# TensorE in place of SyncE waits, behind its loop, until a batched matmul's stores are complete

## The chip, the core and the metric

The kernel runs on one core of a Trainium2 chip. The metric is the device time of one execution in microseconds (us), and less is better. A core has five engines with an instruction stream each: TensorE (PE, with its weight loads shown as PEld), VectorE (DVE), ScalarE (ACT), GpSimd (POOL) and SyncE (SP), which in this kernel issues every DMA. The engines meet only through semaphores. An execution ends when all five are through.

## The reference

The kernel multiplies 32 pairs of float32 matrices: x[b] is 256 by 512 and y[b] is 512 by 384.

```python
batch, dim_i, dim_j, dim_k = 32, 256, 512, 384
return np.einsum('bij,bjk->bik', x, y).astype(np.float32)
```

It reads 41.94 MB and writes 12.58 MB.

## The kernel before

**Tiling.** The 32 matrices are worked off as N = 8 groups of Q = 4. A group lies in SBUF with 32 partitions for each of its four matrices. TensorE multiplies in float16, 32 rows by 128 columns at a time, so that the four matrices of a group use four bands of the array. Each group is done in NE = 2 halves of the rows of x, and each half is 16 steps (T = 16) of four products. Eight banks of PSUM hold the results of both halves.

**Who does what.** SyncE loads group n+2 of x (L69) and y (L73) when GpSimd has cast the same buffer's earlier group. GpSimd casts x and y to float16 (L126, L136). VectorE transposes x (L156) and takes five of sixteen blocks of each result half from PSUM to SBUF (L165); ScalarE takes the other eleven (L165). TensorE runs two nested hardware loops, over the 8 groups and over their 2 halves (L231, L232); the products stand at L217, and each wait in them is a `take` (L214), a wait that also takes the counted value back from its semaphore.

**Stores.** All results have a place of their own in SBUF, and SyncE stores them in three pieces (L96): groups 0 to 4, groups 5 and 6, and group 7. The third piece waits for the last copies of ScalarE and VectorE (L108 and the line behind it). Each store adds 16 to the semaphore s_out when its data has landed.

**The end.** The streams are written out by hand, engine by engine. Behind its third store SyncE raises s_sp (L110), and GpSimd, which waits for it, sets the program's other semaphores to zero (L145) and is through. SyncE's last instruction waits until s_out has 48, and takes the 48 back (L111):

```python
    store(N - 1, N)
    sp.sem_inc(s_sp, 1)
    sp.wait_op(s_out, 16 * 3, "sem-ge").then_inc(s_out, -16 * 3)
```

VectorE and ScalarE end with their last copy, TensorE with the branch of its outer loop. No instruction of the program brings the five engines together at its end.

Of the kernel before, what the change touches and what calls it, by code (L numbers as in the profile page):

```python
# [19 lines left out]
def kernel(  # L20
# [41 lines left out]
    s_out = nc.alloc_semaphore("s_out")  # L62
# [28 lines left out]
    sp = nc.sync  # L91
# [16 lines left out]
    sp.wait_ge(s_dve, NE)  # L108
    store(N - 1, N)
    sp.sem_inc(s_sp, 1)  # L110
    sp.wait_op(s_out, 16 * 3, "sem-ge").then_inc(s_out, -16 * 3)  # L111

# [96 lines left out]
    te = nc.tensor  # L211

    def take(sem):
        te.wait_op(sem, 1, "sem-ge").then_inc(sem, -1)  # L214

    def product(ps, w, m, start, stop, g):
        return te.add_instruction(  # L217
            mybir.InstMatmult(
                name=nc.get_next_instruction_name(),
                start_tensor_calc=start,  # L220
                stop_tensor_calc=stop,
                tile_size=(PQ, P),
                tile_position=(PQ * g, 0),
                engine=mybir.EngineType.PE,
                ins=[te.lower_ap(m), te.lower_ap(w)],
                outs=[te.lower_ap(ps)],
            )
        )

    xt = xt_sb.bitcast(MM_DT).rearrange("p t (m c) -> p t m c", c=2)  # L230
    with te.Fori(0, N):  # L231
        with te.Fori(0, NE) as e:  # L232
            take(s_act)
            take(s_dve)
            for t in range(T):
                if t % STEP == 0:
                    take(s_yr)
                    take(s_xt)
                for g in range(Q):
                    s = slice(g * PQ, (g + 1) * PQ)  # L240
                    ins = product(
                        o_ps[:, e * Q + g, :K],
                        xt[s, t // 2, :, t % 2],
                        y_r[s, t],
                        t == 0,
                        t == T - 1,
                        g,
                    )
                    if t == T - 1 or (g == Q - 1 and t % STEP == STEP - 1):
                        ins.then_inc(s_pe, 1)  # L250


# [28 lines left out]
```

## Time and profile before

| what | value |
|---|---|
| device time, median of 3 runs | 131.95 us (131.85 to 132.28) |
| the profiled execution's own time | 132.13 us |
| its span, first to last instruction of the program | 130.8 us |
| mean granted TensorE clock | 0.823 |
| DMA, mean over the span | 417 GB/s |
| busy: TensorE, VectorE, ScalarE, GpSimd | 47%, 63%, 64%, 57% of the span |

The profile is one execution. Its span runs from the first to the last instruction that belongs to the program; the device time also holds what the engines do around the program, and the two differ by 1.33 us here. Waits, branches and DMA issues are instructions of an engine's sequencer (its name is then PEldq, SPq, ACTq and so on), and they don't count as busy. A wait's start is the moment when it was released. The page cuts the span into 40 slices of about 3.3 us; a digit is a busy share in tenths.

### The profile page before, as it was taken

Reading aid. Unit: us, or ns where it says so; the run is one execution under the profiler, and the core shown is the slowest. Engines: PE = TensorE matmul, PEld = TensorE weight load, DVE = VectorE, ACT = ScalarE, POOL = GpSimd, SP = SyncE. Lnnn points to the kernel's source line nnn. Section 1 sums busy time; section 2 is a strip of 40 time slices with the busy share of each in tenths; the row PEclk is TensorE's granted clock in tenths of the full one; section 3 lists DMA queues with packets and bytes.
Section 4 is the critical chain, followed back from the end, with each engine's and each line's share of the span. In section 5 each row is a group of like instructions: output and inputs, shape, how many; then the busy total and the mean of one; then the engine's idle time right before and its main releaser. Section 6 shows DMA issues by size and latency. Waiting matters only on the chain. (4 is left out here: it accounts for less than half of the span.)

```text
span 130.8 us, 3199 instructions
## 1 busy us (share of the span) xinstructions
PE 61.4 (47%) x1024; PEld 46.7 (36%) x1024; DVE 82.7 (63%) x144; ACT 84.1 (64%) x178; POOL 74.2 (57%) x42
## 2 busy tenths in 40 slices
PE   0000009910992589089329905980975499100000
PEld 0000009800991566046129604970953236000000
DVE  0000036899379999985997997599999957920000
ACT  0400000599659989993998899399999957994000
POOL 0006991199929965992899459758973970000000
PEclk9999999995589689977986985599599959965555
DMA  5999999999999999999999999999999999999995
GB/s 120 451 396 441 421 431 451 443 408 428 451 413 421 438 443 401 436 436 443 423 458 398 443 408 466 398 418 436 463 398 408 427 438 425 436 428 421 425 440 248
DMA packets 3379, 54.55 MB, mean 417 GB/s; under 512 B 304, under 2 KB 304, under 8 KB 304
## 3 DMA queue, kind: packets, MB, share of 16 engines
q1 hardware_dynamic: 3376, 54.53, 98.1%
q14 instruction: 3, 0.02, 0.0%
HBM read 41.94 MB, written 12.58 MB: 417 GB/s over the span
## 5 line engine op out<-in xcount | busy, mean ns | idle before, releaser
L165 ACT COPY o_sb<-o_ps (+1 forms) x176 | 82.6, 469 | 31.7 <-PE o_ps L217 29.6
L217 PE MATMUL o_ps<-y_r,xt_sb 32*128 32x384 f16 x1024 | 61.4, 384 | 50.4 <-PEq L214 49.5
L217 PEld LDWEIGHTS o_ps<-y_r,xt_sb 32*128 32x128 f16 x1024 | 46.7, 107 | 64.6 <-issue 56.8
L156 DVE STREAM_TRANSPOSE xt_sb<-x_r 128x256 f32<-128x256 f32 x64 | 38.1, 626 | 30.9 <-POOL x_r L126 18.4
L136 POOL CAST y_r<-y_sb 128x1536 f16<-128x1536 f32 (+1 forms) x22 | 44.3, 2049 | 15.8 <-DMA y_sb<-in_y_dram 15.3
L165 DVE COPY o_sb<-o_ps 32x384 f32 (+1 forms) x80 | 44.6, 557 | 1.6
L126 POOL CAST x_r<-x_sb 128x2048 f16<-128x2048 f32 x16 | 30.2, 1893 | 16.8 <-DVE o_sb L165 12.1
L202 ACT ACT_TABLE_LOAD x1 | 1.3, 1283 | 3.4 <-PEq L78 3.4
L265 POOL MEMSET const-float32-0.0<- 128x1 f32 x1 | 0.1, 98 | 0.2 <-issue 0.2
L202 ACT COPY spare<-const-float32-0.0 1x1 f32<-1x1 f32 x1 | 0.2, 190 | 0.0
L265 POOL MEMSET const-bfloat16-1.0<- 128x1 bf16 x1 | 0.1, 101 | 0.0
L265 POOL MEMSET const-uint8-127<- 128x1 uint8 x1 | 0.1, 101 | 0.0
L265 POOL MEMSET const-float32-1.0<- 128x1 f32 x1 | 0.1, 98 | 0.0
## 6 DMA issues: line engine op xcount, KB each, us to landing
y_sb<-in_y_dram SPq DMA_DIRECT2D x8, 3072.0 KB, 16.8
x_sb<-in_x_dram SPq DMA_DIRECT2D x8, 2048.0 KB, 17.0
out_dram<-o_sb SPq DMA_DIRECT2D x1, 7680.0 KB, 33.9
out_dram<-o_sb SPq DMA_DIRECT2D x1, 3072.0 KB, 17.3
out_dram<-o_sb SPq DMA_DIRECT2D x1, 1536.0 KB, 11.5
```

The lines of the kernel that those rows point to most:

```text
L126: po.tensor_copy(x_r[:, e], x_sb[n % 2][:, e * H : (e + 1) * H]).then_inc(s_cast, 1)
L136: ins = po.tensor_copy(y_r[:, s], y_sb[n % 2][:, s])
L156: v.transpose(xt_w[:, w], words[:, e, w]).then_inc(s_xt, 1)
L165: ins = copy(o_sb[g * PQ : (g + 1) * PQ, n, e, h], o_ps[h * PQ : (h + 1) * PQ, e * Q + g, :K],)
L202: a_.copy(spare, nc.const_aps.tensor(0.0, [1, 1], F32))
L217: return te.add_instruction(mybir.InstMatmult(name=nc.get_next_instruction_name(), start_tensor_calc=start, stop_tensor_calc=stop, tile_si ...
L265: nc = _bacc.Bacc("TRN2", target_bir_lowering=False, num_devices=1)
```

## The change

SyncE's last instruction is taken away, and the same wait, with the same value and the same taking back, is put behind TensorE's two loops. SyncE then ends with the raising of s_sp, and GpSimd's clearing stays as it is.

```diff
     store(N - 1, N)
     sp.sem_inc(s_sp, 1)
-    sp.wait_op(s_out, 16 * 3, "sem-ge").then_inc(s_out, -16 * 3)
...
                     if t == T - 1 or (g == Q - 1 and t % STEP == STEP - 1):
                         ins.then_inc(s_pe, 1)
+    te.wait_op(s_out, 16 * 3, "sem-ge").then_inc(s_out, -16 * 3)
```

The last line stands outside both loops and runs once.

## The prediction

> **What bounds the kernel now.** I read the page first: its span, its slices and its DMA rows.
>
> ```profile
> span 130.8 us, 3199 instructions
> ...
> PE   0000009910992589089329905980975499100000
> ...
> PEclk9999999995589689977986985599599959965555
> DMA  5999999999999999999999999999999999999995
> ...
> q1 hardware_dynamic: 3376, 54.53, 98.1%
> ```
>
> The DMA row is the one to read: 9 in every slice but the first and the last, while TensorE's row is 0 in the last five. The queue's packets took 98.1% of the span of sixteen DMA engines. The kernel is bound by moving its 54.53 MB, and the change moves no byte and no issue of a DMA. So it can only touch the end. For the end I read the stretches of the tail:
>
> ```profile
> core 0: us, PE busy (x) PEld busy (x) DVE busy (x) ACT busy (x) POOL busy (x), PEclk, DMA share, GB/s
> ...
> 105.90:119.30 13.40, 5.82 (x96) 3.14 (x96) 7.25 (x13) 10.86 (x24) 1.13 (x1) 0.75 1.00 427
> 119.30:130.80 11.50, 0.00 (x0) 0.00 (x0) 0.00 (x0) 0.00 (x0) 0.00 (x0) 0.50 0.89 380
> ```
>
> From 119.3 us on no engine computes; the DMA share is 0.89 and the granted clock of TensorE 0.50. The last 11.5 us are the third store. SyncE's own waits say who stands there:
>
> ```profile
> SPq L111 <- SPq L111: 11.1, 1, 11.1
> SPq L108 <- DVE o_sb L165: 5.0, 1, 5.0
> ```
>
> The longest of the end is SyncE's 11.1 us at L111, the wait that moves. The page's chain of work ends with a ScalarE copy at 119.2 us and doesn't show this; the waits of the DMA queue's own engine do. The lines around it, one by one:
>
> ```profile
> L111 SPq EVENT_SEMAPHORE  x1: 17/17/17, 130.8 to 130.8; - x1
> ```
>
> ```profile
> L110 SPq EVENT_SEMAPHORE  x1: 17/17/17, 119.7 to 119.7; - x1
> ```
>
> ```profile
> L96 SPq DMA_DIRECT2D out_dram<-o_sb x3: 345/390/403, 85.9 to 119.3; - x3
> ...
> DMA to landing us min/median/max: 11.5/17.3/33.9
> ```
>
> The three stores are issued by 119.3, s_sp is raised at 119.7, and SyncE's last wait is released at 130.8 and takes 17 ns. It is the last instruction of the span. The profiled execution's own time is 132.13 us, so 1.33 us lie around the span. Who arrives there when is what the change alters.
>
> **The change part by part.** *Taken from SyncE:* one wait of 17 ns at the very end. SyncE is then through at 119.7 us, 11.1 us sooner. Nothing is queued behind it, and the landing of the stores doesn't depend on it.
>
> *Added to TensorE:* the same wait behind its loops. When does TensorE come to it?
>
> ```profile
> L231 PEldq ALU_OP  x8: 36/36/36, 25.6 to 110.6; - x8
> L231 PEldq COMPARE_BRANCH  x8: 76/208/214, 25.7 to 110.6; - x8
> ```
>
> ```profile
> L217 PEld LDWEIGHTS o_ps<-y_r,xt_sb x1024: 90/93/148, 19.4 to 111.3; 32*128 32x128 f16 x171
> L217 PE MATMUL o_ps<-y_r,xt_sb x1024: 318/322/523, 19.4 to 111.4; 32*128 32x384 f16 x171
> ```
>
> The last branch of the outer loop starts at 110.6, and the last products start at 111.4 and take 0.32 us. These products were handed over ahead of the branch, so the wait stands behind them and holds nothing up; no instruction of the program is queued behind it. TensorE waits there for about 20 us, in which it had nothing to do anyway. What a wait costs on TensorE stands in its loop, with SyncE beside it at the opening barrier:
>
> ```profile
> L214 PEldq EVENT_SEMAPHORE  x160: 51/51/51, 3.9 to 109.9; - x160
> ```
>
> ```profile
> L265 SPq EVENT_SEMAPHORE  x1: 17/17/17, 0.7 to 0.7; - x1
> L265 ACTq EVENT_SEMAPHORE  x1: 17/17/17, 0.7 to 0.7; - x1
> L265 DVEq EVENT_SEMAPHORE  x1: 21/21/21, 0.7 to 0.7; - x1
> L265 PEldq EVENT_SEMAPHORE  x1: 51/51/51, 0.7 to 0.7; - x1
> ```
>
> 160 waits of TensorE take 51 ns each, the least as much as the most, through stretches with a granted clock of 1.00 and of 0.50. SyncE's take 17. So the end of the span moves by 51 - 17 = 34 ns. Two times of the trace's semaphore records, which no view prints, add to this. A semaphore's last rise and the start of the wait that it releases lie 17 ns apart for SyncE at L111 (130,767 and 130,784 ns) and 28 or 29 ns for TensorE in its loop (for instance 107,069 for a rise at 107,041): 11 ns more. **First term: 34 + 11 = 45 ns**, inside the span.
>
> *What comes behind the span.* The semaphore records go on after it. Semaphore 2 isn't the program's; it rises in the opening and at the end. Its rises near the end, in ns from the span's start, from the trace's records:
>
> ```
> 111912 119360 120402 120446 130937 130981 131020 131054 131101
> 131895 131929 131967 132011 132035 132133 132171 132206 132252
> ```
>
> Between the two rows of nine, from 131,063 to 131,671, some 230 other semaphores change once each: they are set back. I read each row as a barrier through which the five engines go one by one, up and back: five steps up, four back. The first row says who is who. TensorE's last product raised its semaphore at 111,751, and 111,912 is the first step. ScalarE's last copy raised its own at 119,256, and 119,360 is the second. GpSimd's clearing starts at 119.7 and takes 163 ns:
>
> ```profile
> L145 POOLq EVENT_SEMAPHORE_RANGE_CLEAR  x1: 163/163/163, 119.7 to 119.7; - x1
> ```
>
> and 120,402 is the third. The fourth, 44 ns later, is then VectorE, which had been through since 115.2. The fifth, at 130,937, is SyncE, 136 ns after its wait ended at 130,801. So the order is TensorE, ScalarE, GpSimd, VectorE, SyncE, and back. SyncE comes last in this order **and** last in time: four steps back are all that is left, 131,101 - 130,937 = 164 ns. If TensorE, the first in the order, comes last in time, the other four still have to step behind it. The second row shows such a full pass, since there everybody waits for TensorE's first step: 132,252 - 131,895 = 357 ns. **Second term: 357 - 164 = 193 ns.** Its bounds are 0, if the order is not what I read, and 357.
>
> *TensorE's way from its wait to the barrier.* SyncE needed 136 ns. TensorE never did just this, so I bound it. From the end of the wait to the next signal at the program's own barriers (L78, semaphore 96) TensorE needed 121 ns (3,100 to 3,221) and SyncE 83 (3,054 to 3,137): 38 ns more, or 1.46 times as much, 174 to 198 ns. From its last product's rise to its barrier step it needed 161 ns, from a standing start. The far row is GpSimd's, 537 ns from the clearing's end (119,865) to 120,402. I take 186, next to the rows of TensorE's own: **third term: 186 - 136 = 50 ns**, with ends at 25 and 401.
>
> The setting back that follows is the same work. Its last part runs until 131,671 on the semaphores 8 to 53, after TensorE is let go at 131,101, and TensorE's step opens the second barrier. TensorE is let go last before and after, so this part shifts and doesn't change.
>
> **The sum:** 45 + 193 + 50 = 288 ns, or 0.29 us, 0.22%. Against the profiled execution: 132.13 + 0.29 = 132.42, with a span of 130.85. The profiled execution is 0.18 above the median of the runs shown; on the median it is 131.95 + 0.29 = **132.24 us**.
>
> The Trainium skill, "Runtime: NRT & Kernel Launch", section "The ~15µs preamble/postamble breakdown", has a serpentine barrier over five engines at 44 ns a step, eight steps, 355 ns. The trace agrees, with 357. By its even steps the second term would be 4 x 44 = 176 ns and the sum 0.27 us.
>
> What can be told from no change in this kernel is about 0.3%, 0.4 us. My forecast is a small loss below that.
>
> **The rivals.** *A, the other side: slower by over 0.3%.* The mechanism is TensorE's way from its wait to its barrier step. It decides from 0.40 - 0.045 - 0.193 = 0.16 us more than SyncE's 0.136, that is from about 0.30 us. If it were as long as GpSimd's 537 ns, the third term would be 401 ns and the sum 0.64: 132.59 us. For it: every instruction of TensorE's sequencer that can be compared is slower than SyncE's (51 to 17, 121 to 83). Against it: at 111,912 TensorE made this very step 161 ns after its last product. What speaks half for it is that part of this way may have been done beside the products, between 110.7 and 111.7.
>
> *B: only the span's 45 ns count.* The device time might stop ahead of the barrier's steps, or the order might not be what I read. Then it is 131.95 + 0.05 = 132.00. For it: I don't know where in the records the 1.33 us begin and end. Against it: with 130.8 of span and 132.13 in all, the clearing of semaphores (to 131.67) and most of the second barrier fit inside.
> [...]
>
> *C: faster.* SyncE may have closing work of its own that now lies beside the third store. From its wait's end to the end of the first setting back by the semaphores 207 to 255, which follow its step, are 131,151 - 130,801 = 350 ns. If TensorE cost nothing and all of this had been on the path, 131.60. Against it: SyncE's share ends ahead of the last one, at 131,671, so hiding it brings nothing.
>
> *D: the change doesn't do what it says*, if TensorE's wait were inside a loop or passed early. The diff has it behind both loops, and s_out reaches 48 only with the third store; if it passed early, TensorE's end would stand near 111 us and the span at 119.9.
>
> **How the numbers follow.** Forecast, a loss of 0.2 to 0.4 us: 0.60, of which about 0.07 are measured beyond 0.4, since the runs of before alone spread over 0.43 us. A: 0.22. B: 0.13, within 0.3%. C: 0.05, of which 0.04 beyond 0.3%. D: well below 0.01, left out of the count. So faster 0.04, within 0.3% 0.53 + 0.13 + 0.01 (the rest of C) = 0.67, slower 0.07 + 0.22 = 0.29. The range reaches from B's 132.00, less 0.10 for the low end of the runs shown (131.85 against 131.95), which is 131.90, to A's 132.59 with as much on top, 132.70; C and the far ends of A stay out.
>
> **What would show it.** In the changed profile TensorE's wait should be the last instruction, of 51 ns, some 28 ns behind the last rise of s_out, and SyncE's last one the raising of s_sp. Between its end and the first of the last nine-step pass I expect 186 ns, and the first pass should last about 357 ns with TensorE's step first and late. The profiled time less the span should grow from 1.33 to about 1.57 us. DMA's row should be the same, digit for digit nearly. If the store's landing moves by more than a few tenths, it is noise of the transfers, not the change. I am wrong if the pass is no longer than 164 ns (the order is read wrongly) or if TensorE's way to it is over 0.30 us.

## The result, and the profile after

The changed kernel takes 132.39 us (median of 10 runs, 132.23 to 133.0) against 131.95 us before (131.85 to 132.28). The ratio is 1.0035, with a 95% interval of 1.0024 to 1.0046: slower by 0.32 to 0.61 us. The profiled execution took 132.25 us, with a span of 130.6 us. Its page, with the rows that were shown of before:

```profile
span 130.6 us, 3199 instructions
...
PE   0000009920992589089419944990985399200000
...
PEclk9999999995589689977985699599599959965555
DMA  5989999999999999999999999999999999999996
...
q1 hardware_dynamic: 3376, 54.53, 98.2%
```

The DMA row is full again in all but its ends and one slice at 8, and the queue's share is 98.2% (98.1% before): the stretch that bounds the kernel is the same. The tail, as stretches:

```profile
core 0: us, PE busy (x) PEld busy (x) DVE busy (x) ACT busy (x) POOL busy (x), PEclk, DMA share, GB/s
...
105.90:119.30 13.40, 5.85 (x96) 3.15 (x96) 7.30 (x13) 11.04 (x24) 1.16 (x1) 0.75 1.01 431
119.30:130.60 11.30, 0.00 (x0) 0.00 (x0) 0.00 (x0) 0.00 (x0) 0.00 (x0) 0.50 0.89 381
```

No engine computes behind 119.3 us, at the same clock and the same DMA share of 0.89. SyncE's own waits have lost their row of 11.1 us:

```profile
SPq L108 <- DVE o_sb L164: 4.9, 1, 4.9
SPq L96 <- ACT o_sb L164: 4.1, 1, 4.1
```

What SyncE ends with, what TensorE ends with, and the stores, by line (the change shifts the lines of TensorE's loop by one):

```profile
L110 SPq EVENT_SEMAPHORE  x1: 17/17/17, 119.7 to 119.7; - x1
```

```profile
L250 PEldq EVENT_SEMAPHORE  x1: 51/51/51, 130.6 to 130.6; - x1
```

```profile
L96 SPq DMA_DIRECT2D out_dram<-o_sb x3: 345/389/403, 86.3 to 119.3; - x3
...
DMA to landing us min/median/max: 11.3/17.1/33.4
```

And the rows that say when TensorE came to its wait, its outer loop's branch and its waits within the loop, and when GpSimd was through:

```profile
L230 PEldq COMPARE_BRANCH  x8: 76/208/214, 25.8 to 110.7; - x8
```

```profile
L213 PEldq EVENT_SEMAPHORE  x160: 51/51/51, 3.8 to 109.9; - x160
```

```profile
L216 PE MATMUL o_ps<-y_r,xt_sb x1024: 318/321/523, 19.5 to 111.5; 32*128 32x384 f16 x171
```

```profile
L144 POOLq EVENT_SEMAPHORE_RANGE_CLEAR  x1: 161/161/161, 119.7 to 119.7; - x1
```

TensorE left its loop at 110.7 us, its last products started at 111.5 (111.4 before), its waits take the same 51 ns, and GpSimd cleared the other semaphores at 119.7 as before. SyncE is through at 119.7. TensorE's wait, 51 ns long, is the last instruction, at 130.6. The third store takes 11.3 us to land, against 11.5, and starts at the same 119.3. So the span is not longer in this execution, it is shorter by 0.16 us (130,801 to 130,645 ns), since the store landed earlier. And yet the time is 0.12 us longer: what lies around the span went from 1.33 to 1.60 us. The records of semaphore 2 in the changed kernel, in ns from the span's start:

```
130880 130914 130952 130996 131019 131116 131155 131189 131236
132021 132056 132094 132137 132161 132258 132296 132331 132377
```

Before, the first four engines had taken their steps by 120.4 us and waited. Now nothing stands there: all nine steps come behind TensorE's, in 356 ns, as long as the second pass (356).

| piece, ns | before | after | predicted |
|---|---|---|---|
| last rise of s_out to the end of the wait | 34 | 79 | 79 |
| end of the wait to that engine's step | 136 | 235 | 186 |
| that step to the end of the first pass | 164 | 356 | 357 |
| end of the first pass to the second's first step | 794 | 785 | unchanged |
| second pass | 357 | 356 | unchanged |

The pieces add up to 326 ns more, 0.33 us or 0.25%, of which 0.28 lie behind the span.

The records also show where the device time ends, which the prediction left open in its rival B. Counted from the span's start, the profiled execution's own time agrees within 10 ns with the sixth of the nine steps of the second pass, here (132,133 ns for 132.13 us before, 132,258 ns for 132.25 us after) and in each of the eight profiles behind the experiments below. So the device time holds the first pass, the setting back and most of the second pass, and moves with them.

### The profile page after: what moved, and what is told of

Same layout as the page of the kernel before. It is cut to its first block, busy times and chain, and to the rows that moved or that the text cites. A ratio compares the mean times of both kernels' runs of the same rounds, so it can differ in the third digit from the quotient of the medians.

```text
span 130.6 us, 3199 instructions
## 1 busy us (share of the span) xinstructions
PE 62.8 (48%) x1024; PEld 46.0 (35%) x1024; DVE 82.7 (63%) x144; ACT 84.4 (65%) x178; POOL 74.2 (57%) x42
## 3 DMA queue, kind: packets, MB, share of 16 engines
q1 hardware_dynamic: 3376, 54.53, 98.2%
## 5 line engine op out<-in xcount | busy, mean ns | idle before, releaser
L216 PE MATMUL o_ps<-y_r,xt_sb 32*128 32x384 f16 x1024 | 62.8, 389 | 49.0 <-PEq L213 49.0
L216 PEld LDWEIGHTS o_ps<-y_r,xt_sb 32*128 32x128 f16 x1024 | 46.0, 108 | 65.4 <-issue 56.1
## 6 DMA issues: line engine op xcount, KB each, us to landing
out_dram<-o_sb SPq DMA_DIRECT2D x1, 1536.0 KB, 11.3
```

What stands on the lines that cost most here:

```text
L216: return te.add_instruction(mybir.InstMatmult(name=nc.get_next_instruction_name(), start_tensor_calc=start, stop_tensor_calc=stop, tile_si ...
```

## Experiments

My theory after this: the whole cost is TensorE's slower wait (45 ns), its longer way to the barrier (99 ns) and its first place in the barrier's order (192 ns). Two rivals: that TensorE's long wait also slows the stores, since 0.46 us were measured and the pieces give 0.33; and that the order means nothing and only TensorE's slowness counts.

### The kernel before as a second program

No edit.

> The kernel before, unchanged, as a second program: it gives the spans of ten executions, which the runs of before did not list, and the size of a difference that means nothing. Both theories: ratio 1.000, within 0.001; time less span 1.33 us in every execution; span about 130.6 to 130.9.

Measured: ratio 0.9999 (0.9987 to 1.0011). The mean span of 12 executions is 130.65 us, that of 35 executions of before beside them 130.71; time less span is 1.35 and 1.34 us (1.28 to 1.41 over all of them; the spans are listed to 0.1 us). What lies around the span scatters little more than the rounding of the spans allows; nearly all the scatter of the time is in the span.

### The changed kernel once more

No edit.

> The changed kernel once more. Theory (the whole cost is TensorE's wait and its first place in the closing barrier): time less span 1.60 us in every execution, span longer than that of the kernel before by 0.045 us, together 0.32 us and a ratio of 1.0025. Rival (TensorE's long wait also slows the stores inside the span): time less span 1.60 as well, but the span longer by about 0.2 us, ratio 1.0035 or more.

Measured: ratio 1.0020 (1.0008 to 1.0032). Mean span 130.69 us over 12 executions against 130.71; time less span 1.63 us against 1.34. In its records TensorE's way to its step is 234 ns and the pass 356 (235 and 356 the first time). The rival, with a span longer by 0.2 us, falls here: TensorE's wait costs nothing inside the span that the mean of the spans can show. That mean can't show the 0.045 us of the theory either; they rest on the records. In the first measurement the changed kernel's mean span was 130.82 us (130.6 to 131.4). The spans of before beside it aren't on record; against the 130.71 here it is 0.11 us longer, about as much as its 0.46 us go beyond the 0.33. Both intervals hold 0.25%.

### TensorE waits long, but SyncE comes last

The first two stores count on a semaphore of their own, and TensorE waits for these alone.

```diff
-        sp.dma_start(out=groups, in_=src).then_inc(s_out, 16)
+        sp.dma_start(out=groups, in_=src).then_inc(s_out if first == N - 1 else s_early, 16)
...
-    sp.wait_op(s_out, 16 * 3, "sem-ge").then_inc(s_out, -16 * 3)
+    sp.wait_op(s_out, 16, "sem-ge").then_inc(s_out, -16)
...
+    te.wait_op(s_early, 16 * 2, "sem-ge").then_inc(s_early, -16 * 2)
```

> TensorE waits for the first two stores alone and SyncE keeps the wait for the third, so TensorE waits long but comes to the barrier ahead of SyncE. Theory (only who comes last counts): time less span 1.33 us, span as before, ratio 1.000. Rival (the long wait of TensorE has a price in itself): ratio about 1.001 or more, with the price in the span.

Its two waits, by line, TensorE's first:

```profile
L252 PEldq EVENT_SEMAPHORE  x1: 51/51/51, 127.1 to 127.1; - x1
```

```profile
L112 SPq EVENT_SEMAPHORE  x1: 17/17/17, 130.8 to 130.8; - x1
```

TensorE is released at 127.1 us and takes its step at 127,453 ns, three others follow within 115 ns, and SyncE ends the barrier: step at 130,948, end of the pass at 131,112, the 164 ns of before. Ratio 1.0005 (0.999 to 1.0021), time less span 1.34 us. So behind the span TensorE's long wait has no price; coming last has. Inside the span a small price isn't excluded: the interval still holds the rival's 1.001, and the mean span of 130.77 us against 130.71, over executions that run from 130.5 to 131.4, doesn't decide it.

### ScalarE, VectorE and GpSimd wait instead

The same wait is put behind ScalarE's last copy, VectorE's last copy or GpSimd's clearing, and away from SyncE, for instance:

```diff
-    sp.wait_op(s_out, 16 * 3, "sem-ge").then_inc(s_out, -16 * 3)
...
+    a_.wait_op(s_out, 16 * 3, "sem-ge").then_inc(s_out, -16 * 3)
```

> ScalarE instead of SyncE waits for all three stores, behind its last copy. Theory (place in the barrier's order, TensorE, ScalarE, GpSimd, VectorE, SyncE and back): seen from ScalarE's step 323 ns are left against SyncE's 164, and its way from the wait to its step is 104 to 136 ns; time less span 1.46 to 1.49 us, span plus 0.00 to 0.01, ratio 1.001. Rival (the order doesn't matter, TensorE is only slow): ScalarE's instructions are as short as SyncE's, so time less span 1.33 and ratio 1.000.

> VectorE waits for all three stores, behind its last copy. Theory (place in the order): behind VectorE's step 241 ns of the barrier are left (164 for SyncE, 325 measured for ScalarE, 356 for TensorE), its way to the step is 110 to 150 ns; time less span 1.40 to 1.45 us. Rival (every engine but SyncE pays the same for a late end): 1.52 as with ScalarE, or 1.60 as with TensorE.

> GpSimd waits for all three stores, behind its clearing of the other semaphores. Theory: 285 ns are left behind its step. If its way to the step is as short as ScalarE's (150 ns), time less span is 1.46 to 1.50 us; if the 537 ns that lay between the clearing and its step in the kernel before are GpSimd's own way at any time, 1.85 us, and GpSimd is dearer than TensorE although it stands later in the order.

The waits themselves, ScalarE's, VectorE's and GpSimd's, one from each kernel:

```profile
L210 ACTq EVENT_SEMAPHORE  x1: 17/17/17, 130.7 to 130.7; - x1
```

```profile
L191 DVEq EVENT_SEMAPHORE  x1: 21/21/21, 130.7 to 130.7; - x1
```

```profile
L145 POOLq EVENT_SEMAPHORE  x1: 17/17/17, 130.6 to 130.6; - x1
```

ScalarE's and GpSimd's waits are as short as SyncE's, 17 ns, and VectorE's is 4 ns longer, so the wait itself explains next to nothing of what follows. Each kernel's pieces, in ns from the records, with SyncE and TensorE beside them, in the order of the barrier:

| engine that ends last | wait's end to its step | its step to the end of the pass | time less span, us |
|---|---|---|---|
| TensorE | 235 | 356 | 1.60 |
| ScalarE | 150 | 325 | 1.51 |
| GpSimd | 566 | 287 | 1.88 |
| VectorE | 196 | 250 | 1.48 |
| SyncE | 136 | 164 | 1.33 |

The third column falls from row to row, as the theory says (323, 285 and 241 were expected in the middle rows, and all three came within 9 ns): the later an engine stands in the order, the less is left behind it. The records show the order itself, too: one, two and three steps stand early, ahead of the late engine's, with ScalarE, GpSimd and VectorE last. Against SyncE's row the two columns add up to 0.29, 0.18, 0.55 and 0.15 us more for TensorE, ScalarE, GpSimd and VectorE, and time less span grows by 0.27, 0.18, 0.55 and 0.15. The rival without an order expected 1.33 us with ScalarE and falls, and so does the one by which every engine but SyncE pays the same. ScalarE's mean time less span is 1.52 us over 12 executions; its ratio of 1.0011 (0.9996 to 1.0026) alone couldn't tell the theory from the rival. My sizes of the second column were off: ScalarE took 150 ns where I had 104 to 136 (so its 1.51 us missed my 1.46 to 1.49), VectorE 196 where I had 110 to 150 (so its 1.48 us missed my 1.40 to 1.45), and GpSimd took the long way when it came last, too: 566 ns, against 537 in the kernel before. One execution each stands behind VectorE and GpSimd.

### A second wait on the engine that ends last

Both kernels get a further wait, released already:

```diff
+    te.wait_op(s_out, 16 * 3, "sem-ge").then_inc(s_out, -16)
+    te.wait_op(s_out, 16 * 2, "sem-ge").then_inc(s_out, -16 * 2)
```

and the same with `sp` in SyncE's stream, each in place of the one wait.

> The kernel before with two waits of SyncE in place of one, the second released already: one more sequencer instruction on the engine that ends last. If what stands behind the wait on that engine counts fully, the span's end moves by one instruction of SyncE, 0.03 to 0.08 us behind the last rise of s_out, and time less span stays 1.34 us.

> The changed kernel with two waits of TensorE in place of one, the second released already. Theory (TensorE's sequencer is the slower one, instruction by instruction, and it is on the path): the second wait starts 150 ns behind the first, as two waits in its loop do, so the end of the span lies 0.15 us later behind the last rise of s_out, and time less span stays 1.63 us. Rival (the longer way from wait to barrier is a fixed cost of the engine and not of its instructions): 0.05 us or less.

TensorE's two waits by line, and then SyncE's two:

```profile
L250 PEldq EVENT_SEMAPHORE  x1: 51/51/51, 131.3 to 131.3; - x1
```

```profile
L251 PEldq EVENT_SEMAPHORE  x1: 51/51/51, 131.5 to 131.5; - x1
```

```profile
L111 SPq EVENT_SEMAPHORE  x1: 17/17/17, 130.6 to 130.6; - x1
```

```profile
L112 SPq EVENT_SEMAPHORE  x1: 17/17/17, 130.7 to 130.7; - x1
```

In the records TensorE's second wait starts 151 ns after its first (131,331 and 131,482), and SyncE's 67 ns after its first (130,610 and 130,677). From the last rise of s_out to the end of the span are 230 ns (79 with one wait) and 101 ns (34 with one). Time less span stays at 1.62 and 1.34 us, and TensorE's way from its last wait to its step stays at 235 ns. So a further wait behind the landing of the last store counts in full, and on TensorE it counts over twice as much. The rival's 0.05 us or less falls for an added wait; whether TensorE's 235 ns to its step are made of such slow instructions isn't shown. The times themselves, 133.15 and 132.03 us, are single executions; in the first the last store landed late, at 131.3 us, and the second wait is only 0.15 us of its distance to 132.39.

## Why the prediction was right, point by point

- **The bound.** Right: the DMA row is the same but for two slices, by one digit each, and the mean spans before and after, measured side by side, are alike (130.71 and 130.69 us).
- **First term, 45 ns.** Right to the nanosecond: 79 ns in place of 34 from the last rise to the end of the wait. The clock of 0.50 in the tail didn't lengthen TensorE's 51 ns.
- **Second term, 193 ns.** Right: 356 - 164 = 192. The order that was read out of one profile, from which engine ended when, was borne out by moving the wait to each of the five engines.
- **Third term, 50 ns.** The mechanism was right, the size wrong: TensorE needed 235 ns where I took 186, 99 more than SyncE, inside the ends of 25 and 401. I had sized it by TensorE's own barrier rows and by its 161 ns behind the last product. A part of the way may have been done beside the products there; that is argued, no run separates it.
- **The sum, 0.29 us.** The records give 0.33, the two measurements 0.46 (0.32 to 0.61) and 0.26 us (0.11 to 0.42). The predicted 132.24 us is 0.15 below the 132.39 measured, which lies inside the stated range. Of this, 0.04 us are the pieces (the third term is 49 ns over, the others together 11 under); the rest seems to lie in the spans of that measurement, and its cause isn't shown. I called a loss under 0.3% the likeliest. The first measurement lies just over that bound, where rival A had it but without rival A's cause, and the second under it: on which side one comparison falls is chance here.
- **Rival A**, TensorE's way over 0.30 us, is wrong for TensorE (235 ns) and true of GpSimd (566 ns): the place that I named, at another engine. **Rival B**, the span's 45 ns alone, is wrong: 0.28 us lie behind the span. **Rival C** is wrong: SyncE's setting back, read as that of the semaphores 207 to 255, still comes behind its own step (131,141 to 131,225 ns, with the step at 131,019), so an early end saves it nothing. **Rival D** is wrong by the wait's row at 130.6.

What lies around the span isn't the same for every kernel: it was 1.33 us with SyncE last and 1.88 with GpSimd last. The even step of 44 ns that the Trainium skill, "Runtime: NRT & Kernel Launch", section "The ~15µs preamble/postamble breakdown", gives for the barrier ahead of a kernel is right here for the whole closing pass (8 x 44 = 352, measured 356), not for each step: in the passes of these two kernels they run from 23 to 98 ns.

No version beats the kernel before: of the five engines SyncE is the cheapest to end with, in both columns of the table.

What stays open: why the way from the wait to the step is so unlike from engine to engine (136 to 566 ns); why TensorE's way was 270 ns in the kernel where it came to the barrier at 127 us (127,183 to 127,453), with the third store still landing, and 234 or 235 ns in the three where it came last; and why the span was longer by 0.1 us in the mean of the first ten executions of the changed kernel and not of the next twelve, against the same 130.71.

## What to carry to other kernels

The engine whose stream ends last sets what comes behind the program's last instruction: leave the last wait to the engine with the least left behind it, here SyncE, and put nothing behind that wait. An engine that idles at the end isn't free if it is slow to get from its wait to the closing barrier, or stands early in that barrier's order. A difference of a few tenths of a per cent is read from the pieces of a profile, and from time less span over many executions, not from two medians.

## What the runs showed that I had not expected

GpSimd needs 566 ns from the end of its last wait to its step in the closing barrier, four times as long as SyncE (136), though its wait takes the same 17 ns. And what lies around the span is so even that it tells more than the times do: 1.28 to 1.41 us, mean 1.34, over 35 executions of before with spans rounded to 0.1 us, while their times run from 131.79 to 132.79.
